# Layer A's passes two to four on half-precision parts of normalised tokens

## The chip, the core and the metric

The kernel runs on one core of one Trainium2 chip. A core has TensorE (PE in the profile; PEld is its loading of weights), VectorE (DVE), ScalarE (ACT), GpSimd (POOL) and SyncE (SP), which here issues every transfer between the chip's memory (DRAM) and the on-chip memory (SBUF); matmuls write to PSUM banks. The metric is the device time of one execution in microseconds (us); lower is better.

## The reference

Two layers process 2048 prompt tokens and 64 sample tokens of width 1024. Each layer is

```python
h = rms_norm(x, norm_g)              # x * rsqrt(mean(x*x) + eps) * g
q, k, v, gate = split(h @ w_in)
q, k = rms_norm(q, q_g), rms_norm(k, k_g)      # per head of 64
o = attend(q, k, v, bias, valid, sinks)
x = x + (o * silu(gate)) @ w_out
```

Layer A has 16 heads of queries on two heads of keys and values; a token sees its own chunk of 64 and two chunks before it, with a bias by distance and a sink per head. Layer B has 16 heads of everything and sees eight chunks back. The outputs are the two results and the newest keys and values.

## The kernel before

**Tiles and units.** Tokens lie along the free dimension in DRAM (`x0`, 128 partitions x 8 blocks x 2112 tokens). A unit is 256 tokens (two tiles of 128); eight units hold the prompt and a ninth the sample. Layer A makes four passes (`qd` 0 to 3) over the units. A pass projects queries and gates of four heads (512 columns); pass one (`qd` 0) also projects keys and values (256 columns). That is 68 tiles in all, 17 in a pass.

**Precision.** A product is made of three matmuls of parts: high x high, high x low, low x high (`project`, L753 to L755; the sample unit has both parts in one operand, L748 and L749). In layer A the parts are 32-bit values in the matmul's reduced format (`fp32r`, written f32 in the profile's PE rows). `load_act` splits raw tokens: a cast on ACT (L634) makes the high part, a subtraction on POOL (L635) the low part. Weights are multiplied by the norm's gain and split in `load_weights` (L537 on ACT, L540 on DVE). The token's 1/rms (`rr`) is applied behind the projection, when a bank of PSUM is read (`evacuate`, `evacuate_a`). Layer B's parts are half precision (f16): tokens are multiplied by their 1/rms before the split (`token_rows`, L709, spreads them over the partitions with PE; L631 multiplies on DVE), and the weights are brought to a common size by a factor from a scan of their largest value (`scan`, L177, and `input_top`, `input_across`, `input_scales`).

**What passes share.** The parts of a unit's tokens are written to a buffer in DRAM (`xsa`) and read by the passes behind. By `KEEP` units 0 and 1 are split twice, in passes one and two, and written in the second; the other units are split and written in pass one.

**Order.** PE's instructions run in an order written out by hand. `pipeline` in `layer_a` goes through the tiles: in step i come the scores of tile i, the outputs of tile i-1, and between them pieces of the projection of tile i+3 (`filler.to`). The other engines' and SP's instructions are placed by a scheduler. Small jobs that wait (`bg`) are run between the pieces. A projection bank (`pj`, two of them) is free when `evacuate_a` has read the gate (L793) and, behind the sum of squares (L840) and the power on POOL (L844), the product of L847 has read the q part.

Of the kernel before, what the change touches and what calls it, by code (L numbers as in the profile page):

```python
# [17 lines left out]
P = 128  # L18
# [24 lines left out]
FR = 0.6  # L43
KEEP = [1, 1] + [0] * (NU - 1)

# [12 lines left out]
def hybrid_encoder_kernel(  # L58
# [97 lines left out]

    most = const([P, 84], "most")
    top = const([P, 12], "top")
    scl = const([P, 9, 4], "scl")
    gsb = const([P, 8, KC], "gsb")  # L160
    S_W, C_B, G_B, C_T = (lambda h, i=i: scl[:, h, i : i + 1] for i in range(4))
    S_WO, S_OG, C_O = (scl[:, 8, i : i + 1] for i in range(3))
# [4 lines left out]
    def scan_source(i):  # L167
        if i < 64:
            return w_in_b[i // 8, i % 8 // 2, :, i % 2, :]
        if i < 80:  # L170
            return w_o_b[(i - 64) // 8, i % 8 // 2, :, i % 2, :]
        return cv_b[2 * (i - 80) : 2 * (i - 80) + 2].rearrange("e p c h d -> p e (c h d)")

    def scan(i=None, keep=0):
        while len(pending) > keep:
            j, raw = pending.pop(0)
            r = nc.vector.tensor_reduce(  # L177
                most[:, j : j + 1], raw, axis=AX.X, op=ALU.max, apply_absolute_value=True
            )
            if r.ins.engine in bg.anchors:  # L180
                behind(r.ins, bg.anchors[r.ins.engine])
            scanned.append(j)
        if i is not None:
            raw = t("wraw", [P, 512], WB) if keep else t("scan", [P, 512], 1)
            dst = raw if i < 80 else raw.rearrange("p (e c) -> p e c", e=2)
            behind(load(dst, scan_source(i)).ins, held["last"])
            pending.append((i, raw))
# [90 lines left out]
    def input_scales(h):  # L278
        everywhere(h, row[:, 20:24])

    def output_top():
# [137 lines left out]
    x1 = dr.tile([P, KC, TOK], F32, tag="x1", name="x1")  # L419
    xs = [dr.tile([P, 2 * KC * TOK], dt, tag=n, name=n) for n, dt in (("xsa", F32), ("xsb", F16))]  # L420

# [154 lines left out]
    def load_act(  # L576
# [17 lines left out]

        if cached and dt == F16:
# [6 lines left out]
            return x  # L602
        if cached:
            for c in range(4):
                xx = t("xx", [P, 4 * OT], XN, dt)
                held["last"] = load(wide(xx[:, : 4 * T]), kept(c)).ins
                x.parts.append(parts_of(xx, T, joint))
            return x

        def fetch():  # L610
# [7 lines left out]
        def split(c):  # L618
            def fn():
# [22 lines left out]
                x.parts.append(parts)  # L642
                if cache is not None and dt == F32R:
                    store(kept(c), wide(xx[:, : 4 * T]))
                elif cache is not None and c % 2:
# [33 lines left out]

    rr = [const([P, NT + 1], f"rms{l}") for l in range(2)]  # L680

    def token_scales(unit, x, ps):
# [7 lines left out]
    def sums_to_scales(layer, tt, parts, ps):  # L690
        w = len(parts)
        for i, part in enumerate(parts):
            nc.tensor.matmul(ps[:, 2 * i : 2 * i + 2], part, ones, start=True, stop=True)
# [10 lines left out]

    def token_rows(unit):
        _, T, tiles = unit
        ps = tp_bank()
        for i, (tt, _, _) in enumerate(tiles):
            nc.tensor.matmul(  # L709
                ps[:, i * P : (i + 1) * P], rr[1][:, tt : tt + 1].to_broadcast([P, P]), ident,  # L710
                start=True, stop=True,
            )
        rows = t("rows", [P, UT], 1)
        nc.vector.tensor_scalar(rows[:, :T], ps[:, :T], HB, 1.0, op0=ALU.mult, op1=ALU.mult)
        return rows

    def row_scales(unit):
        _, T, tiles = unit
        w = len(tiles)
        tt = tiles[0][0]  # L720
        acc = t("ms", [P, 8])
        for i, (_, t0, n) in enumerate(tiles):
# [38 lines left out]

    def evacuate(layer, tt, n, ps, C, G, b=None):
        a = t("pa", [P, 384], 4)
# [7 lines left out]
        else:  # L771
            out = a
        sc = rr[layer][:, tt : tt + 1]
        for dst, src in pieces:
# [10 lines left out]

    def evacuate_a(tt, ps, C, G):
        a = t("pa", [P, 384], 4)
        b = t("pb", [P, 256], 5) if G else a[:, P : 2 * P]
        sc = rr[0][:, tt : tt + 1]
        w = 2 * P if G else P  # L790
# [285 lines left out]
    def layer_a():  # L1076
# [4 lines left out]
        def add_unit(qd, place, unit):  # L1081
# [30 lines left out]
            def take_kv(it, ps):  # L1112
                tt, t0, n = it.tile
                last = u == NU
                it.kv = pr = evacuate(0, tt, n, ps, 256, 0)
                kn, v = pr[:n, 0:128], pr[:n, 128:256]
# [15 lines left out]
            def take_qg(it, ps):  # L1132
                tt, t0, n = it.tile
                if n == P and (qd or unit is not order[0]):
                    it.pr, it.gate, norm = evacuate_a(tt, ps, 512, 256)
                else:
                    it.pr, it.gate = evacuate(0, tt, n, ps, 512, 256)
                    norm = head_norm(n, it.pr[:n, 0:256], qd > 0)
# [283 lines left out]
        def outputs(it):  # L1422
# [18 lines left out]
            finished[key] = finished.get(key, 0) + 1  # L1441

        def pipeline():
            N = len(items)
            for i in range(-3, N + 1):
# [5 lines left out]
                if 0 <= i < N:  # L1451
# [58 lines left out]
    def layer_b():  # L1510
# [4 lines left out]
        def add_unit(hp, unit):  # L1515
# [7 lines left out]
            def prefetch():  # L1523
                for j in range(NO):
                    assert finished["x1", j] == 2 or j * OT >= u * UT + T
                rows = None if hp else token_rows(unit)
                st.x[hp, u] = x = load_act(
# [680 lines left out]
```

## Time and profile before

| what | value |
|---|---|
| median of three timed runs | 2076.58 us (2071.28 to 2080.74) |
| span of the profiled execution | 2081.5 us; its own time around the span is not recorded |
| attention of layer A, first to last gate row (L1361) | 54.75 to 680.04 us |
| PE, granted clock over the span | 0.994 |
| matmul groups of L753, L754, L755 with f32 operands, 512 columns | 220.8, 203.6, 203.8 us busy |
| DMA, one queue on SP | 426.51 MB, 79.9% of 16 engines |

A row of instructions reads: line, engine, operation, what is written <- what is read, shapes, count, then busy us, mean ns of one, and the engine's idle time just before with what ended it. Matmuls overlap: a mean of 398 ns is a latency, and the pace is the distance of two starts.

### The profile page before, as it was taken

The page shows a single profiled execution, that of the slowest core. Times are in us where ns is not written, and L with a number is a line of the kernel's source. Part 1 is how long each engine was busy: PE and PEld are TensorE (multiplying, and loading weights), DVE is VectorE, ACT ScalarE, POOL GpSimd, SP SyncE. Part 2 cuts the span into 40 slices and gives each one's busy share as a digit, 9 for nine tenths or more (in the row PEclk, how much of TensorE's full clock was granted, in tenths as well). Part 3 has the DMA queues.
Part 4 walks back from the last instruction along what each step waited for, and adds up shares of the span by engine and source line. Part 5 has one row for each costly group of instructions (what it writes and reads, how often), then busy time and mean ns, then how long its engine had stood idle before and what let it go on. Part 6 is the DMA issues. An engine that isn't in the chain of part 4 may idle for free.

```text
span 2081.5 us, 40775 instructions
## 1 busy us (share of the span) xinstructions
PE 1994.4 (96%) x12814; PEld 1429.3 (69%) x12814; DVE 1405.7 (68%) x4073; ACT 1439.1 (69%) x3572; POOL 1133.0 (54%) x1529
## 2 busy tenths in 40 slices
PE   7898999999999999989999999999999999999999
PEld 6777788777888999745555555555555555557888
DVE  7666777767667555677767676676766767667542
ACT  6777888777788433367778677787877778687430
POOL 5665565454447445578556565665756656565000
PEclk9999999999999999999999999999999999999999
DMA  8878787899766666789889789797987979678763
GB/s 259 252 209 220 218 213 184 228 232 240 210 159 177 197 215 204 265 227 248 218 184 244 167 200 222 175 238 176 201 221 171 245 163 215 154 155 200 229 198 113
DMA packets 610712, 429.11 MB, mean 206 GB/s; under 512 B 404208, under 2 KB 547968, under 8 KB 610464
## 3 DMA queue, kind: packets, MB, share of 16 engines
q1 hardware_dynamic: 610496, 426.51, 79.9%
q8 instruction: 101, 1.65, 0.3%
q14 instruction: 115, 0.94, 0.1%
HBM read 257.59 MB, written 73.43 MB: 159 GB/s over the span
## 4 chain that ended last, share of the span: by engine, by line
PE 54%; DVE 8%; ACT 6%; DMA 5%; issue 4%; POOL 2%; SPq 1%; ACTq 0%; DVEq 0%; POOLq 0%
PE pj L753 9%; PE pj L755 9%; PE pj L754 9%; PE o L1840 4%; PE pj L2051 4%; PE pj L2053 4%; PE pj L2052 4%; PE sb L1678 2%; PE sb L1679 2%; PE tp L1006 1%; DMA pt<-values 1%; DVE p L1682 1%; DVE wh L540 1%; DMA wraw<-in_w_o_a_dram 1%; POOL xx L635 1%
## 5 line engine op out<-in xcount | busy, mean ns | idle before, releaser
L753 PE MATMUL pj<-wh,xx 128*128 128x512 f16 (+2 forms) x1648 | 642.5, 390 | 22.4 <-DVE pa L847 9.6
L755 PE MATMUL pj<-wh,xx 128*128 128x512 f16 (+2 forms) x1648 | 624.0, 379 | 0.6 <-POOL xx L635 0.6
L1735 POOL TENSOR_TENSOR values<-p,values 128x640 f16<-128x640 f32 (+4 forms) x256 | 327.3, 1279 | 205.5 <-ACT values L1734 199.1
L754 PE MATMUL pj<-wh,xx 128*128 128x512 f16 x1024 | 388.3, 379 | 1.3 <-DVE wh L540 1.3
L1694 ACT ACTIVATE p<-p,nm 128x640 f32<-128x640 f32 (+5 forms) x264 | 199.5, 756 | 180.0 <-DVE nm L1687 141.0
L2051 PE MATMUL pj<-xx,wh 128*128 128x264 f32 (+1 forms) x1024 | 290.5, 284 | 11.2 <-DVE res L2057 4.0
L1682 DVE CUSTOM_DVE_ANT_0 p<-sb,BT 128x640 f32<-128x640 f32 (+5 forms) x272 | 196.5, 722 | 150.2 <-PE sb L1679 129.3
L2052 PE MATMUL pj<-xx,wh 128*128 128x264 f32 (+1 forms) x1024 | 287.6, 281 | 0.0
L635 POOL TENSOR_TENSOR xx<-xraw,xx 128x528 fp32r<-128x528 f32 (+4 forms) x144 | 184.7, 1304 | 100.2 <-ACT xx L634 92.9
L754 PE MATMUL pj<-wl,xx 128*128 128x512 f32 (+1 forms) x624 | 235.4, 377 | 2.4 <-DVE wl L540 2.4
L844 POOL TENSOR_TENSOR f<-f,mhalf 128x4 f32<-128x4 f32 x182 | 186.3, 1024 | 12.2
L755 PEld LDWEIGHTS <-xx 128*128 128x128 f16 x1024 | 100.2, 98 | 123.7 <-issue 1.9
L1342 ACT ACTIVATE p<-p,nm 128x257 f32<-128x257 f32 (+2 forms) x272 | 134.4, 496 | 70.5 <-DVE nm L1331 35.8
L1495 POOL TENSOR_TENSOR o<-gt,o 128x256 f32<-128x256 f32 (+1 forms) x132 | 104.9, 794 | 142.2 <-ACT p L1342 72.0
L1734 ACT CAST values<-p 128x640 f16<-128x640 f32 (+4 forms) x256 | 168.2, 658 | 12.5 <-DMA pt<-values 6.5
L754 PEld LDWEIGHTS <-xx 128*128 128x128 f16 x1024 | 100.3, 98 | 83.5 <-issue 3.6
L753 PEld LDWEIGHTS <-xx 128*128 128x128 f16 x1024 | 100.3, 98 | 82.0 <-ACT sq L822 1.4
L1840 PEld LDWEIGHTS <-values 128*128 128x128 f16 x1344 | 123.3, 98 | 38.8 <-DMA pt<-values 2.7
L753 PEld LDWEIGHTS pj<-wh,xx 128*128 128x128 f32 x624 | 119.7, 192 | 40.3 <-issue 8.1
L2053 PE MATMUL pj<-xx,wl 128*128 128x264 f32 x512 | 145.8, 285 | 0.9 <-DVE wl L533 0.9
L1840 PE MATMUL o<-pt,values 128*128 128x256 f16 (+1 forms) x1344 | 143.7, 255 | 1.7 <-DMA pt<-values 1.3
L2053 PE MATMUL pj<-xx,wh 128*128 128x264 f16 x512 | 141.3, 276 | 1.4 <-DVE wh L530 1.4
(292 smaller groups left out, 4719.8 us busy)
## 6 DMA issues: line engine op xcount, KB each, us to landing
xx<-xsb SPq DMA_DIRECT2D x112, 512.0 KB, 4.3
xx<-xsa SPq DMA_DIRECT2D x88, 512.0 KB, 5.0
xraw<-oga SPq DMA_DIRECT2D x64, 264.0 KB, 3.6
xraw<-ogb SPq DMA_DIRECT2D x64, 264.0 KB, 4.0
xsa<-xx SPq DMA_DIRECT2D x32, 512.0 KB, 4.0
wl<-in_w_in_b_dram SPq DMA_DIRECT2D x64, 256.0 KB, 4.9
wraw<-in_w_in_b_dram SPq DMA_DIRECT2D x56, 256.0 KB, 3.5
xraw<-in_x_dram SPq DMA_DIRECT2D x40, 256.0 KB, 4.6
```

Source lines behind the costliest of these rows:

```text
L635: nc.gpsimd.tensor_tensor(lo, rv, wide(hi), op=ALU.subtract)
L753: nc.tensor.matmul(ps[:n, :C], xh, wh, start=k == 0, stop=False)
L754: nc.tensor.matmul(ps[:n, :C], xh, wl, start=False, stop=False)
L755: nc.tensor.matmul(ps[:n, :C], xl, wh, start=False, stop=k == KC - 1)
L844: nc.gpsimd.tensor_tensor(fv, fv, mhalf[:n, :H], op=ALU.pow)
L1682: mi = nc.vector.tensor_tensor_reduce(out=p[r, :nk], in0=S[r, o : o + nk], in1=b, op0=ALU.add, op1=ALU.min, scale=1.0, scalar=3e38, accum_ ...
L1694: ex = nc.scalar.activation(p[:n, :nk], p[:n, :nk], AF.Exp, scale=-1.0, bias=it.nm[:n, c : c + 1], accum_out=it.sm[:n, c : c + 1],)
L1735: lo = nc.gpsimd.tensor_tensor(two[:, :, 1, :], pv, two[:, :, 0, :], op=ALU.subtract)
L1840: nc.tensor.matmul(it.O[:, h * T + q0 : h * T + q1_], held["VH"][:, kt, h], x, start=kt == kb and not low, stop=kt == tb and low == 1,)
L2051: nc.tensor.matmul(ps[:, :OT], wh, oh, start=k == 0, stop=False)
L2052: nc.tensor.matmul(ps[:, :OT], wh, ol, start=False, stop=False)
L2053: nc.tensor.matmul(ps[:, :OT], wl, oh, start=False, stop=k == KC - 1)
```

## The change

Passes two to four read f16 parts of tokens that are already multiplied by their 1/rms. 36 conversions (nine units, four pieces of two blocks each) make these parts: a load of raw tokens, a multiply on DVE, a cast on ACT, a subtraction on POOL and a store to `xsa`, which is f16 now. `pipeline` calls one or two of them a step from the second tile on, in the order in which pass two takes the units; a unit that is not there when its load is due is converted then. Pass one splits tokens as before, but writes nothing. Two 512 KB loads of a unit's parts take the place of four.

The weights of passes two to four are scanned on the chip, one of 24 pieces a step, for their largest value; `first_top`, `first_across` and `first_scales` make the factor for a pass. The weights are split into f16 with gain times factor, and the projection's bank is read with a constant in place of the token's scale. A smaller on-chip scratch for dynamic transfers makes room.

```diff
-KEEP = [1, 1] + [0] * (NU - 1)
...
+        if i >= 84:
+            return w_qg_a[(i - 76) // 8, (i - 84) % 8 // 2, :, i % 2, :]
...
+    def first_top(q):
+        a = 76 + 8 * q
+        mv = most[:, a : a + 8]
+        nc.vector.tensor_tensor(mv, mv, gain[:, 0, :], op=ALU.mult)
+        largest(10 + q, a, a + 8)
+
+    def first_across(q):
+        ps = tp_bank()
+        nc.tensor.transpose(ps[0:1, 0:P], top[:, 10 + q : 11 + q], ident)
+        m, e, r, o = (row[:, 48 + i : 49 + i] for i in (0, 1, 2, 4))
+        nc.vector.tensor_reduce(m, ps[0:1, 0:P], axis=AX.X, op=ALU.max)
...
+    def first_scales(q):
+        ps = tp_bank()
+        nc.tensor.matmul(
+            ps[:, 0:2], ones[0:1, 0:1].to_broadcast([1, P]), row[:, 52:54], start=True, stop=True
+        )
+        nc.vector.tensor_copy(scl[:, 8 + q, 0:2], ps[:, 0:2])
+        times(gsa[:, q], gain[:, 0, :], scl[:, 8 + q, 0:1])
...
-        if cached:
-            for c in range(4):
-                xx = t("xx", [P, 4 * OT], XN, dt)
-                held["last"] = load(wide(xx[:, : 4 * T]), kept(c)).ins
...
-                if cache is not None and dt == F32R:
-                    store(kept(c), wide(xx[:, : 4 * T]))
...
+    def convert(unit, c):
+        u, T, tiles = unit
+        o, joint = u * UT, T == TS
+        if c == 0 and held.get("rowed") != u:
+            rows_of(unit)
+
+        def fn():
+            raw = t("yraw", [P, 2 * UT], 2)[:, : 2 * T].rearrange("p (k s) -> p k s", k=2)
+            ld = load(raw, x0[:, 2 * c : 2 * c + 2, o : o + T])
+            behind(ld.ins, held["last"])
+            nc.vector.tensor_tensor(
+                raw, raw, held["rows"][:, :T].unsqueeze(1).to_broadcast([P, 2, T]), op=ALU.mult
+            )
+            both = t("x16", [P, 4 * UT], 3, F16)
+            xh, xl = parts_of(both, T, joint)
+            hi, lo = (xh[:, :, :T], xh[:, :, T:]) if joint else (xh, xl)
+            nc.scalar.copy(hi, raw)
+            nc.gpsimd.tensor_tensor(lo, raw, hi, op=ALU.subtract)
+            a = o * 2 * KC + 4 * c * T
+            store(xs[0][:, a : a + 4 * T], both[:, : 4 * T])
...
-                cache = None if qd < KEEP[u] else xs[0]
-                st.x[qd, u] = x = load_act(x0, u * UT, T, sums, T == TS, lead, cache, qd > KEEP[u])
+                if qd:
+                    while ("x", u) not in known:
+                        converts(1)
+                    st.x[qd, u] = x = load_act(x0, u * UT, T, False, T == TS, None, xs[0], True, F16)
+                    return x
+                st.x[qd, u] = x = load_act(x0, u * UT, T, sums, T == TS, lead)
...
-                    (st.w[qd],), _, st.emit[qd] = load_weights(0, (w_qg_a[qd], 512))
+                    (st.w[qd],), _, st.emit[qd] = load_weights(1, (w_qg_a[qd], 512), scale=gsa[:, qd])
...
+                sc = C_A(qd) if qd else rr[0][:, tt : tt + 1]
...
+        def ahead(i):
+            if 0 <= i < 24:
+                scan(84 + i)
...
                 filler.to(c0 + 0.3 * (end - c0))
+                ahead(i)
...
+                if i > 0:
+                    converts(1 + (i % 3 == 0))
...
-    nc = _bacc.Bacc("TRN2", target_bir_lowering=False, num_devices=1)
+    nc = _bacc.Bacc("TRN2", target_bir_lowering=False, num_devices=1, dynamic_dma_scratch_size=1024)
```

More of the change, by code (lines that the diff above doesn't have):

```diff
@@ L279, in input_scales @@
         everywhere(h, row[:, 20:24])
+    def first_top(q):
[8 more added lines that the diff above has]
+        nc.vector.tensor_reduce(m, ps[0:1, 0:P], axis=AX.X, op=ALU.max)
+        nc.vector.tensor_scalar(m, m, 1e-12, 1.0, op0=ALU.max, op1=ALU.mult)
+        powers(m, e, r)
+        times(o, r, WB_)
+        times(row[:, 53:54], e, 1 / (HB * WB_))
+    def first_scales(q):
[5 more added lines that the diff above has]
+        times(gsa[:, q], gain[:, 0, :], scl[:, 8 + q, 0:1])
+    C_A = lambda q: scl[:, 8 + q, 1:2]
     def output_top():
@@ L419, in hybrid_encoder_kernel @@
     x1 = dr.tile([P, KC, TOK], F32, tag="x1", name="x1")
-    xs = [dr.tile([P, 2 * KC * TOK], dt, tag=n, name=n) for n, dt in (("xsa", F32), ("xsb", F16))]
+    xs = [dr.tile([P, 2 * KC * TOK], dt, tag=n, name=n) for n, dt in (("xsa", F16), ("xsb", F16))]
     def wide(x):
@@ L680, in hybrid_encoder_kernel, with rows_of, converts @@
     rr = [const([P, NT + 1], f"rms{l}") for l in range(2)]
+    known = set()
+    def rows_of(unit):
+        held["rowed"] = unit[0]
+        held["rows"] = token_rows(unit, 0)
+    def convert(unit, c):
[17 more added lines that the diff above has]
+            store(xs[0][:, a : a + 4 * T], both[:, : 4 * T])
+        fn()
+    normal = []
+    def converts(n):
+        for _ in range(min(n, len(normal))):
+            unit, c = normal.pop(0)
+            convert(unit, c)
+            if c == 3:
+                known.add(("x", unit[0]))
     def token_scales(unit, x, ps):
@@ L691, in sums_to_scales @@
         w = len(parts)
+        known.update((layer, tt + i) for i in range(w))
         for i, part in enumerate(parts):
@@ L720, in row_scales @@
         tt = tiles[0][0]
+        known.update((0, tt + i) for i in range(w))
         acc = t("ms", [P, 8])
@@ L1441, in outputs @@
             finished[key] = finished.get(key, 0) + 1
+        normal.extend((unit, c) for unit in order[2:5] + order[:2] + order[5:] for c in range(4))
+        def ahead(i):
+            if 0 <= i < 24:
+                scan(84 + i)
+            elif i == 24:
+                scan()
+            q, at = divmod(i - 1, 8)
+            if i > 0 and 1 <= q <= 3:
+                if at == 0:
+                    first_top(q)
+                elif at == 1:
+                    first_across(q)
+                elif at == 2:
+                    first_scales(q)
+                    known.add(("w", q))
+            if i > 0 and normal and normal[0][1] == 0:
+                rows_of(normal[0][0])
         def pipeline():
```

37 lines of the change are left out of this document (18 added, 19 removed).

## The prediction

> **What bounds the kernel now.** I read the page's head first, then busy times by stretch (start:end, length, then busy us of PE, PEld, DVE, ACT and POOL with counts, the granted clock, the DMA share), and then who made PE wait in the two stages that the change touches. The first stage is pass one of layer A once attention runs, the second is passes two to four; 222 us is taken as the border because projections run three tiles ahead of attention, and the row of the fourteenth gated tile stands there.
>
> ```profile
> span 2081.5 us, 40775 instructions
> PE 1994.4 (96%) x12814; PEld 1429.3 (69%) x12814; DVE 1405.7 (68%) x4073; ACT 1439.1 (69%) x3572; POOL 1133.0 (54%) x1529
> ...
> 221.82 0.62 POOL L1361 TENSOR_TENSOR G<-pb,sm 128x256 f32<-128x256 f32 x1 [3.02 <-DVE sm L1359]
> ...
> 54.00:222.00 168.00, 150.66 (x935) 126.61 (x934) 110.12 (x377) 130.89 (x360) 98.12 (x147) 0.96 0.82 224
> 222.00:640.00 418.00, 409.29 (x2365) 328.85 (x2363) 297.79 (x971) 338.87 (x933) 220.95 (x380) 1.00 0.80 211
> 552.00:627.00 75.00, 75.00 (x438) 61.25 (x437) 50.59 (x174) 60.74 (x167) 36.77 (x64) 1.00 0.69 179
> ```
>
> In 222 to 640, PE is busy 409.29 of 418 us, and in 552 to 627 without a gap, while ACT, next in line, stands at 60.74 of 75 (81%). So passes two to four are bound by PE, and a shorter matmul shortens them. Pass one is looser: 17 us of gaps, and the clock at 0.96. The waits of PE (total us, times, longest), first 54 to 222, then 222 to 640:
>
> ```profile
> PE pj L753 <- DVE pa L847: 8.4, 5, 4.0
> PE pj L753 <- ACT pa L776: 4.1, 1, 4.1
> PE pj L753 <- ACT xx L634: 3.2, 1, 3.2
> ...
> PE o L1403 <- DVE pl L977: 3.9, 10, 0.5
> PE tp L1006 <- DVE pa L847: 1.3, 2, 1.1
> PE o L1403 <- ACT ph L976: 1.2, 1, 1.2
> PE o L1403 <- DMA pt<-values: 0.9, 1, 0.9
> ```
>
> Pass one loses its time where a projection bank comes free late: L847, the scaling of the normed q that reads the bank, comes after POOL's power (L844), and whatever stands ahead of it on POOL or DVE delays the next projection. In the later passes the four waits make 7.3 us.
>
> **The gain: f16 projections.** One run of twelve projection matmuls in layer A, and one in layer B, where both operands are f16 already (start, duration):
>
> ```profile
> 598.38 0.51 PE L753 MATMUL pj<-wh,xx 128*128 128x512 f32 x1
> 598.72 0.40 PE L754 MATMUL pj<-wl,xx 128*128 128x512 f32 x1
> ...
> 601.04 0.40 PE L755 MATMUL pj<-wh,xx 128*128 128x512 f32 x1
> 601.27 0.38 PE L1006 MATMUL tp<-ident,pa 128*128 128x128 f32 x2
> ...
> 1111.13 0.38 PE L753 MATMUL pj<-wh,xx 128*128 128x512 f16 x1
> 1111.35 0.38 PE L754 MATMUL pj<-wh,xx 128*128 128x512 f16 x1
> ...
> 1113.51 0.38 PE L755 MATMUL pj<-wh,xx 128*128 128x512 f16 x1
> 1113.72 0.33 PE L1678 MATMUL sb<-KB,q 128*128 128x384 f16 x1
> ```
>
> From 598.72 to 601.04 are ten starts, 0.232 us each; from 1111.35 to 1113.51 ten, 0.216. The f32 run of twelve lasts 2.89 us, which is 12 x 0.232 and 0.11 more for the switch into f32; the f16 run lasts 2.59, no more than 12 x 0.216. A tile's 24 matmuls stand in three runs, so a tile gains 24 x 0.016 + 3 x 0.11 = 0.7 us. Three passes of 16 tiles give 33 us; the sample tile's 16 matmuls add one, which I leave as rounding. The groups agree (behind the bar: busy us, mean ns of one):
>
> ```profile
> L755 PE MATMUL pj<-wh,xx 128*128 128x512 f16 x1024 | 388.4, 379 | 0.6 <-POOL xx L635 0.6
> L753 PE MATMUL pj<-wh,xx 128*128 128x512 f32 x512 | 220.8, 431 | 17.1 <-DVE pa L847 8.4 <-ACT pa L776 4.9 <-ACT xx L634 3.2
> L755 PE MATMUL pj<-wh,xx 128*128 128x512 f32 x512 | 203.8, 398 | 0.0
> ...
> L754 PEld LDWEIGHTS pj<-wl,xx 128*128 128x128 f32 x624 | 120.3, 193 | 17.5 <-DVE wl L540 3.0
> L754 PEld LDWEIGHTS <-xx 128*128 128x128 f16 x1024 | 100.3, 98 | 83.5 <-issue 3.6
> ```
>
> (52 + 19 + 19 ns over 400 triples would be 36 us.) I take **33**, bounds 31 and 36. The weight load halves, from 193 to 98 ns.
>
> The Trainium skill, "TensorE: Matmul & The Clock Gate" (Step-by-step: what each phase is for), says that a load of weights is pulled ahead under the running matmul. By that rule a load of 193 ns would hide behind a matmul of 216 ns, and the gain would be nothing. The trace disagrees: the f32 starts are 0.232 apart.
>
> **What is added.** Layer B's first pass already makes such parts; its rows price the steps. In order: multiply by the token's scale, cast, low part, scan of weights, token scales spread over partitions by PE.
>
> ```profile
> L631 DVE TENSOR_TENSOR xraw<-xraw,rows 128x512 f32<-128x512 f32 x32 | 25.5, 839 | 0.2
> L634 ACT CAST xx<-xraw 128x512 f16<-128x512 f32 x32 | 18.6, 616 | 12.3 <-DVE xraw L631 9.0 <-DVE ms L695 3.3
> L635 POOL TENSOR_TENSOR xx<-xraw,xx 128x512 f16<-128x512 f32 x32 | 40.4, 1287 | 15.1 <-ACT xx L634 15.1
> L177 DVE TENSOR_REDUCE most<-wraw 128x1 f32<-128x512 f32 x76 | 51.5, 678 | 0.3
> L709 PE MATMUL tp<-ident,rms 128*128 128x128 f32 x34 | 6.0, 299 | 2.3 <-DVE scl L228 1.9 <-DVE scrow L210 0.4
> ...
> 850.00:980.00 130.00, 119.12 (x699) 70.47 (x698) 97.30 (x255) 82.80 (x198) 96.79 (x107) 0.99 0.91 254
> 1110.00:1240.00 130.00, 129.23 (x778) 74.59 (x777) 92.80 (x277) 98.33 (x241) 81.42 (x108) 1.00 0.86 202
> ```
>
> The change makes 36 conversions (DVE 30, ACT 22, POOL 46 us) and 24 scans (DVE 16 us); it drops the second split of units 0 and 1 (8 casts, 8 low parts) from pass two. All lies beside PE except the 17 spreading matmuls (6 us at most) and three small scale pairs. What conversions cost PE through queues, layer B shows: with 36 of them in 850 to 980, PE was busy 119.12 us of 130, later 129.23. The 10 us between is my price for 36, spreading matmuls within.
>
> The pace is four conversions in three tile steps from the first step on: 17 fall in pass one, 19 in the first 14 steps of pass two. The 19 cost 19/36 of 10, **5** us. For the 17 in pass one, that price is 5 too, but ACT there goes from 130.89 to about 141 of 168 us (84%), while it had 64% in 850 to 980, and POOL gets 22 us more ahead of the L844 that frees banks. I take double, **10**; bounds 0 and 17, the last being all of today's gaps once more. Scans and scale pairs: **2**, bounds 0 and 5; the cover is DVE's spare time, 110.12 busy of 168. Queued behind a scan or multiply that waits for its load are, on DVE, the score minimum and L847, then PE.
>
> Later passes have shorter steps: ACT's 81% becomes about 88%, and the wait on pl (3.9 us today) should grow. I take **3**, bounds -3 and 8. DMA helps against that:
>
> ```profile
> xx<-xsa SPq DMA_DIRECT2D x88, 512.0 KB, 5.0
> ...
> xsa<-xx SPq DMA_DIRECT2D x32, 512.0 KB, 4.0
> ...
> xraw<-in_x_dram SPq DMA_DIRECT2D x40, 256.0 KB, 4.6
> ```
>
> 88 loads become 48, and 32 stores become 32 of half the size. New are 32 loads of 256 KB for the conversions and 24 for the scans, while 8 of the 40 loads of x go with the second split, so the sum falls by 20 + 8 - 12 = 16 MB; issues on SP stay near the same number (88 + 32 + 8 against 48 + 32 + 32 + 24), so its queue gains little. Weight splits, evacuations by a constant in place of the token's scale, and smaller scratch cost nothing here: the same instructions on the same engines, beside a PE that is late.
>
> Sum: -33 + 5 + 10 + 2 + 3 = **-13 us**. The span is 2081.5; this execution's time around it is not shown, and the three timed runs (2071.28 to 2080.74, median 2076.58) lie below it, 0.2% at the median. The terms are differences, so I take them from the median: **2063.5**.
>
> **The rivals.**
>
> *Given back in pass one* (chance 0.27). Conversions double pass one's 17 us of gaps and its clock loss (0.04 of 168 is 7), and take the 14 x 0.7 = 10 us that pass two would gain while they last: -33 + 24 + 10 = +1, about **2077**. Rows for it:
>
> ```profile
> 86.47 1.26 POOL L635 TENSOR_TENSOR xx<-xraw,xx 128x512 fp32r<-128x512 f32 x1
> ...
> 86.71 1.30 DVE L938 SCALAR_TENSOR_TENSOR pb<-sq,pb 128x256 f32<-128x256 f32 x1
> ...
> 89.56 0.76 PE L753 MATMUL pj<-wh,xx 128*128 128x512 f32 x1 [4.03 <-DVE pa L847]
> 90.12 0.63 PE L754 MATMUL pj<-wl,xx 128*128 128x512 f32 x1
> ```
>
> A low part on POOL, a DVE product that ends only after it, a bank freed late, a gap of 4.03 us, and matmuls of 0.63 us in place of 0.40 after it. The Trainium skill, "SBUF — State Buffer" (SBUF: two separate sides), gives a rule for it: a DVE instruction with two SBUF inputs and a POOL one exclude each other for the whole instruction. By that rule, the trace agrees (1.30 us at 86.71), and 36 more low parts and 36 multiplies collide more often. Against it: the split's 512 KB stores leave pass one, and with them SP's waits for POOL.
>
> *All hidden* (0.15). The background work fits into idle time, PE keeps its order, and nearly the whole 33 is seen: about **2047**. For it: the shares above stay under 90%; against: 850 to 980.
>
> *Slower: DVE held by loads* (0.05). Its place is DVE's queue: 60 new instructions (36 multiplies, 24 scans) wait for fresh transfers with L847 behind them. At 1 us of PE each the sum is -33 + 60 = +27, **2103**; it passes +0.5% from 0.72 us each. Against: 76 scans in layer B waited 0.3 us in all, 32 multiplies 0.2.
>
> *No faster pace* (0.03). If something of layer A other than its type sets 0.232, the gain is gone and about 17 us remain as cost: **2094**. Against: the weight load halves with the type.
>
> **How the numbers follow.** The forecast has 0.50, with its own range 2055 to 2070. 0.5% is 10.4 us, about what a measurement tells from no change, so the bound of faster is 2066. Faster: 0.38 of the forecast and 0.15; same: 0.12 of the forecast and 0.25 of given back; slower: 0.02, 0.05 and 0.03. The range 2046 to 2081 leaves out the slower cases, the tail of given back and part of all hidden.
>
> **What would show it.** Projections of passes two to four as f16 with starts 0.216 apart, and 552 to 627's step about 0.7 us shorter: the gain. Pass one longer by some 10 us, with more waits on L847: its price. PE's gaps in passes three and four not above 11 us: no new bound. The prediction fails if pass one grows by over 20 us, or if PE idles in passes three and four behind ACT.

## The result and the profile after

The changed kernel takes 2103.59 us (median of four runs, 2100.46 to 2108.02), the kernel before beside it 2075.13 (2071.28 to 2080.74): a ratio of 1.0142, with an interval of 1.012 to 1.0164. It is **slower**, by some 29 us, where 13 us less were forecast: the whole interval lies above 1, though by less than 2%. The time lies above the range.

The head of the page after, and its row of the parts' loads:

```profile
span 2102.1 us, 41007 instructions
...
PE 1990.2 (95%) x12857; PEld 1342.8 (64%) x12857; DVE 1454.7 (69%) x4172; ACT 1452.2 (69%) x3600; POOL 1168.9 (56%) x1557
...
xx<-xsa SPq DMA_DIRECT2D x48, 512.0 KB, 4.8
```

The change does what it says: 48 loads in place of 88, and PE has 4 us less to do. The longer span is time in which PE waits: its gaps sum to 87.1 us of the span before and 111.9 after. Busy times by stretch show where (columns as in the prediction: PE, PEld, DVE, ACT, POOL, clock, DMA share, GB/s). First after, with pass one, passes two to four, and the first 14 steps of pass two; then the same 14 steps before:

```profile
54.00:222.00 168.00, 145.99 (x908) 122.92 (x907) 123.84 (x391) 131.73 (x357) 114.27 (x155) 0.96 0.77 209
222.00:640.00 418.00, 390.47 (x2338) 236.78 (x2336) 320.41 (x1015) 334.62 (x924) 227.55 (x380) 0.98 0.67 173
235.00:363.00 128.00, 115.54 (x680) 68.81 (x679) 105.23 (x328) 100.98 (x276) 81.15 (x124) 0.96 0.79 213
```

```profile
222.00:338.00 116.00, 113.50 (x658) 91.43 (x656) 82.65 (x274) 98.96 (x269) 69.25 (x114) 1.00 0.75 196
```

The 14 steps grew from 116 to 128 us. PE went from 98% busy to 90%, while DVE went from 82.65 us (71%) to 105.23 (82%); ACT's 100.98 is hardly more than before. The granted clock of these steps fell too, from 1.00 to 0.96, but it does not order the kernels: in the same 14 steps e1 below has 0.97 and takes 115.0 us, e4 0.99 and takes 125.8. PE's waits after, 222 to 640 (total, times, longest):

```profile
PE o L1466 <- DVE pl L1034: 8.6, 9, 2.8
PE tp L1063 <- DVE sm L1422: 6.3, 1, 6.3
PE o L1466 <- DMA pt<-values: 4.1, 2, 2.3
```

The two largest end with DVE. Five rows of the timeline around the longest one, of 6.3 us (start, duration, engine):

```profile
291.09 4.88 DVE L568 SCALAR_TENSOR_TENSOR wh<-wl,gsa,wh 128x512 f16<-128x512 f32 x4
...
300.91 1.21 DVE L716 TENSOR_TENSOR yraw<-yraw,rows 128x512 f32<-128x512 f32 x1
...
302.64 0.47 DVE L904 SCALAR_TENSOR_TENSOR pa<-pj,scl,f 128x256 f32<-128x256 f32 x1
...
303.04 0.16 DVE L1422 RECIPROCAL sm<-sm 128x4 f32<-128x4 f32 x1
...
303.26 0.66 PE L1063 MATMUL tp<-ident,pa 128*128 128x128 f32 x2 [6.30 <-DVE sm L1422]
```

PE wants to transpose a tile's queries (pa) and stands still for 6.30 us. The profile names a reciprocal of 0.16 us as what released it; L904, which writes the queries themselves, ended only 0.09 us ahead of it, behind the same burst on DVE. In front of both lie, among the usual work, four low parts of weights, a scan and multiplies of tokens; from 288.00 to 303.20 DVE was busy 15.08 of 15.20 us. DVE has idle time over the stage, but not at this place.

**Stages.** The start of each tile's gate row (before L1361, after L1424) cuts layer A; these are differences of those rows in us, for the kernels whose stages the text uses. Span start to the 14th row is pass one, 14 more rows the part of pass two with conversions, 40 more the rest of layer A; behind the last row comes layer B.

| kernel | to 14th row | next 14 | next 40 | behind | span |
|---|---|---|---|---|---|
| before | 221.8 | 115.9 | 342.3 | 1401.5 | 2081.5 |
| after | 234.6 | 128.5 | 332.0 | 1407.0 | 2102.1 |
| e1, gain alone | 219.4 | 115.0 | 331.5 | 1405.8 | 2071.7 |
| e2, cost alone | 232.1 | 139.2 | 339.5 | 1400.0 | 2110.8 |
| e3, no multiply | 229.0 | 125.0 | 330.8 | 1405.5 | 2090.3 |
| e5, no multiply, no scan | 231.8 | 122.5 | 330.7 | 1402.0 | 2086.9 |
| e8, f16 without added work | 222.6 | 112.4 | 330.7 | 1408.7 | 2074.4 |
| e9, before with low parts moved | 215.7 | 115.2 | 339.7 | 1405.3 | 2075.8 |
| e10, e8 with low parts moved | 215.8 | 114.1 | 326.6 | 1400.5 | 2057.0 |

The profiled execution of before was some 8 us slower than its median, and the times behind layer A differ by up to 9 us over the same code, so small differences of this table are read with that in mind. The medians below carry the verdicts.

### The profile page after: what moved, and what is told of

Its sections match the earlier page's. It is cut to its first block, busy times and chain, and to the rows that moved or that the text cites. A ratio compares the mean times of both kernels' runs of the same rounds, so it can differ in the third digit from the quotient of the medians.

```text
span 2102.1 us, 41007 instructions
## 1 busy us (share of the span) xinstructions
PE 1990.2 (95%) x12857; PEld 1342.8 (64%) x12857; DVE 1454.7 (69%) x4172; ACT 1452.2 (69%) x3600; POOL 1168.9 (56%) x1557
## 4 chain that ended last, share of the span: by engine, by line
PE 57%; DVE 14%; ACT 9%; DMA 8%; issue 7%; POOL 5%; SPq 1%; POOLq 0%; ACTq 0%; DVEq 0%
PE pj L812 10%; PE pj L813 10%; PE pj L814 10%; PE pj L2136 4%; PE pj L2138 4%; PE pj L2137 4%; PE o L1925 4%; PE sb L1763 2%; PE sb L1764 2%; DVE p L1394 2%; PE tp L1063 2%; DMA pt<-values 1%; DVE wh L568 1%; POOL xx L656 1%; DVE o L1579 1%
## 5 line engine op out<-in xcount | busy, mean ns | idle before, releaser
L812 PE MATMUL pj<-wh,xx 128*128 128x512 f16 (+2 forms) x1648 | 626.2, 380 | 30.3 <-DVE pa L904 9.8
L814 PE MATMUL pj<-wh,xx 128*128 128x512 f16 (+2 forms) x1648 | 619.9, 376 | 0.0
L813 PE MATMUL pj<-wh,xx 128*128 128x512 f16 x1408 | 535.6, 380 | 1.3 <-DVE wh L568 1.3
L814 PEld LDWEIGHTS <-xx 128*128 128x128 f16 x1408 | 138.2, 98 | 169.0 <-issue 4.1
L656 POOL TENSOR_TENSOR xx<-xraw,xx 128x528 fp32r<-128x528 f32 (+4 forms) x136 | 177.0, 1323 | 89.1 <-ACT xx L655 82.5
L812 PEld LDWEIGHTS <-xx 128*128 128x128 f16 x1408 | 138.2, 98 | 115.9 <-issue 5.8
L813 PEld LDWEIGHTS <-xx 128*128 128x128 f16 x1408 | 138.2, 98 | 114.5 <-issue 5.7
L1394 DVE CUSTOM_DVE_ANT_0 p<-sa,BT,nsink 128x256 f32<-128x256 f32 (+2 forms) x272 | 116.2, 468 | 7.5 <-PE sa L1384 3.2
L900 POOL TENSOR_TENSOR f<-f,small 128x4 f32<-128x4 f32 x182 | 38.0, 209 | 148.0 <-DVE f L897 129.9
```

Of the source, the lines that this page charges most:

```text
L656: nc.gpsimd.tensor_tensor(lo, rv, wide(hi), op=ALU.subtract)
L812: nc.tensor.matmul(ps[:n, :C], xh, wh, start=k == 0, stop=False)
L813: nc.tensor.matmul(ps[:n, :C], xh, wl, start=False, stop=False)
L814: nc.tensor.matmul(ps[:n, :C], xl, wh, start=False, stop=k == KC - 1)
```

## The experiments

A difference in us is (ratio - 1) x 2073, the median of before in those runs (2071.73 to 2073.99 in three groups).

**Gain and cost apart.** e1 keeps the f16 projections, their loads and as many stores, and takes the work away; e2 keeps the projections of before and does all the work into a buffer that nobody reads.

```diff
 e1, from the kernel after
-            raw = t("yraw", [P, 2 * UT], 2)[:, : 2 * T].rearrange("p (k s) -> p k s", k=2)
-            ld = load(raw, x0[:, 2 * c : 2 * c + 2, o : o + T])
...
-            nc.scalar.copy(hi, raw)
-            nc.gpsimd.tensor_tensor(lo, raw, hi, op=ALU.subtract)
-            store(xs[0][:, a : a + 4 * T], both[:, : 4 * T])
+            st = store(xs[0][:, a : a + 4 * T], x16[:, : 4 * T])
...
-                scan(84 + i)
 e2, from the kernel after
-            store(xs[0][:, a : a + 4 * T], both[:, : 4 * T])
+            store(spare16[:, a : a + 4 * T], both[:, : 4 * T])
...
+                cache = None if qd < KEEP[u] else xs[0]
...
-                    (st.w[qd],), _, st.emit[qd] = load_weights(1, (w_qg_a[qd], 512), scale=gsa[:, qd])
+                    (st.w[qd],), _, st.emit[qd] = load_weights(0, (w_qg_a[qd], 512))
```

> Leaves out the conversions (a constant piece is stored in their place) and the scans (a fixed factor); projections of passes two to four are f16 as in the changed kernel, so the output is not the reference's. Theory (the cost of the background work ate the gain): PE's f16 order alone gains about 0.44 us in each of 48 tile steps, 21 us, less grown waits: 2054 to 2062. Rival (the attention chain between the projections holds the step, whatever the projections cost): passes three and four stay as long as before, 2068 to 2076.

> The kernel before, with f32 projections and its own shared parts, plus all conversions and scans of the change, whose parts go to a buffer that nobody reads. Theory (DVE is too full while the work lasts): pass one and the first 14 steps of pass two grow by 25 us or more, 2098 to 2120. Rival (the f16 steps are too short for work that the longer f32 steps would hide): 2076 to 2088.

e1: 2070.27 us, ratio 0.9991 (0.9978 to 1.0005), 2 us less than before and not told from it. e2: 2113.19, ratio 1.0198 (1.0174 to 1.0223), 41 more. So the background work costs 31 us in the changed kernel (1.0142 against 0.9991), and the gain without it is near nothing. Both are news: the forecast had 17 us of cost (10, 5 and 2) and 33 of gain. e2 minus e1's gain would give 39 where the change gave 29; e2 also moves the f32 parts (DMA 0.91 busy in pass one, after 0.77), so its 41 is no clean price of the work.

**Which work.** e3 is without the multiply of tokens and the spreading of their scales, e4 without the subtraction on POOL; e12 has a fixed factor for the weights in place of the scan, and e5 is e3 and e12 in one.

```diff
 e3 and e5, from the kernel after
-            nc.vector.tensor_tensor(
-                raw, raw, held["rows"][:, :T].unsqueeze(1).to_broadcast([P, 2, T]), op=ALU.mult
-            )
 e4
-            nc.gpsimd.tensor_tensor(lo, raw, hi, op=ALU.subtract)
 e5 and e12
+    for q in range(1, 4):
+        nc.vector.memset(scl[:, 8 + q, 1:2], 0.5 / (HB * WB_))
+        times(gsa[:, q], gain[:, 0, :], 2 * WB_)
...
-            if 0 <= i < 24:
-                scan(84 + i)
```

> Leaves out the multiply by the token's scale in the conversions, and with it the spreading of the scales (passes two to four work on tokens without that scale). DVE loses 36 instructions of about 0.8 us with their waits for the load of x; ACT, POOL and the transfers keep theirs. Theory (DVE's queue): 12 to 20 us faster than the changed kernel, 2084 to 2092. Rival (POOL's low parts ahead of the power that frees a bank): within 5 us of the changed kernel, 2099 to 2104.

> Leaves out the subtraction on POOL in the conversions; the low parts of passes two to four stay zero. Theory (DVE's queue): within 6 us of the changed kernel, 2097 to 2104. Rival (POOL's low parts, by their place ahead of the power and by the port that they share with DVE): 10 to 20 us faster, 2084 to 2093.

> Leaves out the multiply by the token's scale and also the scans (a fixed factor for the weights); conversions keep load, cast, low part and store. Theory (what costs is DVE's time and what waits in its queue): DVE is back near the load of the kernel before, 2072 to 2081. Rival (casts, low parts and transfers of the conversions carry the rest): 2084 to 2089, like the run without the multiply alone.

> The changed kernel with a fixed factor in place of the scans of weights (24 loads of 256 KB, 24 reductions of 0.68 us on DVE, three small chains left out). Theory (cost goes by DVE's time; the multiplies cost 15 us for 30 us of it): 5 to 9 us faster than the changed kernel, 2094 to 2099. Rival (scans fill idle time): 2101 to 2104.

| kernel | median us | ratio to before | us above before |
|---|---|---|---|
| after | 2103.59 | 1.0142 (1.012 to 1.0164) | 29.4 |
| e4, no low parts | 2098.50 | 1.0121 (1.0099 to 1.0144) | 25.1 |
| e12, no scan | 2092.98 | 1.0110 (1.0084 to 1.0136) | 22.8 |
| e3, no multiply | 2088.86 | 1.0083 (1.0062 to 1.0104) | 17.2 |
| e5, neither multiply nor scan | 2082.34 | 1.0038 (1.0020 to 1.0056) | 7.9 |
| e1, none of the work | 2070.27 | 0.9991 (0.9978 to 1.0005) | -1.9 |

By the medians, DVE's share is 21.5 us of the 31.3 (29.4 to 7.9): the multiplies (with the spreading) 12, the scans 7 when taken alone and 9 between e3 and e5. POOL's 46 us of low parts cost about 4. The intervals don't separate these 4 from nothing, nor the 7 of e12; the other steps they do. Casts, low parts and loads together are the remaining 10 (e5 to e1). The time of e5 fell between its two expectations. One row of after, grouped by line from 54 to 363 us, shows the multiplies, one the scans (busy, mean ns, idle before):

```profile
L716 DVE TENSOR_TENSOR yraw<-yraw,rows 128x512 f32<-128x512 f32 (+1 forms) x36 | 26.1, 731 | 11.8 <-DMA yraw<-in_x_dram 11.7
...
L179 DVE TENSOR_REDUCE most<-scan 128x1 f32<-128x512 f32 x24 | 16.2, 675 | 0.0
```

By the medians these 42 us of DVE's time cost 21.5 of the kernel's: about half a microsecond for each, and rather less for DVE alone. With the scans go 24 loads, with the multiplies the spreading matmuls, and the wait for tokens moves to ACT, whose casts wait 9.3 us for them in e5.

The stages give DVE less. The 28th gate row stands at 363.1 us in after, 354.0 in e3, 354.2 in e5 and 334.4 in e1: 9 us for multiplies and scans, 20 for the rest. The profiled execution of e5 took 2088.70 us, 6 more than its median, so its stages may be that much too long, which doesn't close the gap. That the background work costs some 30 us is shown; that most of it is DVE's is not: its share lies between 9 us (stages) and 21 (medians).

**Is it the wait for loads?** The idle 11.7 us of that row are DVE standing at a multiply whose tokens have not landed, which is the mechanism of the rival at 2103. e11 loads the raw tokens two pieces ahead, into four buffers.

```diff
 from the kernel after
+    def fetch_raw():
+        if len(fetched) < len(pieces):
+            (u, T, _), c = pieces[len(fetched)]
+            raw = t("yraw", [P, 2 * UT], 4)[:, : 2 * T].rearrange("p (k s) -> p k s", k=2)
+            ld = load(raw, x0[:, 2 * c : 2 * c + 2, u * UT : u * UT + T])
...
+            while len(fetched) < min(n + 3, len(pieces)):
+                fetch_raw()
```

> The changed kernel with the raw tokens of a conversion loaded two pieces ahead, in four buffers in place of two. Theory (DVE's time is what costs; it stood only 12 us waiting for these loads): 0 to 8 us faster than the changed kernel, 2096 to 2103. Rival (the wait of the multiply at the head of DVE's queue for its load): 15 us faster or more, 2088 or less.

What the multiplies of e11 waited for, in the view of that line (us, times):

```profile
  DMA yraw<-in_x_dram: 4.0, 3
```

The wait fell from 11.7 us to 4.0, and the time did not fall with it: 2106.58, ratio 1.0192 (1.0158 to 1.0227). So that rival named the right time with the wrong mechanism: it had 60 instructions stand for a microsecond each, and they stood for 11.7 us in all. e11 is no clean trade, though: its multiplies took 890 ns on average in place of 731, and its casts waited 4.4 us for a store of earlier parts. What DVE costs is then rather the length of the added work in a fixed order, of which the stall of 6.30 us is one case; no run prices that apart.

**Why the gain is small.** e1 has nothing added and yet gains 2 us. Five gate rows of pass three before (a step is the distance of two rows), with the busy times of this stretch, and the same five tiles after, with theirs:

```profile
423.78 0.61 POOL L1361 TENSOR_TENSOR G<-pb,sm 128x256 f32<-128x256 f32 x1 [2.20 <-DVE sm L1359]
431.49 0.62 POOL L1361 TENSOR_TENSOR G<-pb,sm 128x256 f32<-128x256 f32 x1 [1.48 <-DVE sm L1359]
440.46 0.61 POOL L1361 TENSOR_TENSOR G<-pb,sm 128x256 f32<-128x256 f32 x1 [1.47 <-DVE sm L1359]
448.27 0.62 POOL L1361 TENSOR_TENSOR G<-pb,sm 128x256 f32<-128x256 f32 x1 [1.49 <-DVE sm L1359]
457.24 0.61 POOL L1361 TENSOR_TENSOR G<-pb,sm 128x256 f32<-128x256 f32 x1 [1.47 <-DVE sm L1359]
```

```profile
423.78:457.24 33.46, 32.87 (x191) 26.59 (x189) 23.24 (x76) 25.63 (x73) 16.18 (x28) 1.00 0.89 237
```

```profile
448.63 0.62 POOL L1424 TENSOR_TENSOR G<-pb,sm 128x256 f32<-128x256 f32 x1 [2.21 <-DVE sm L1422]
456.34 0.61 POOL L1424 TENSOR_TENSOR G<-pb,sm 128x256 f32<-128x256 f32 x1 [1.51 <-DVE sm L1422]
465.31 0.61 POOL L1424 TENSOR_TENSOR G<-pb,sm 128x256 f32<-128x256 f32 x1 [1.48 <-DVE sm L1422]
473.12 0.61 POOL L1424 TENSOR_TENSOR G<-pb,sm 128x256 f32<-128x256 f32 x1 [1.49 <-DVE sm L1422]
482.09 0.62 POOL L1424 TENSOR_TENSOR G<-pb,sm 128x256 f32<-128x256 f32 x1 [1.48 <-DVE sm L1422]
```

```profile
448.63:482.09 33.46, 32.07 (x195) 19.58 (x194) 23.23 (x76) 25.62 (x73) 16.08 (x29) 1.00 0.67 150
```

The steps are 7.71, 8.97, 7.81 and 8.97 us in both, to the hundredth, though the conversions have long ended, PE has less to do and DMA fell from 0.89 to 0.67. A step whose length doesn't move when the projections shrink is not set by them, not even with PE at 98%. DVE's and ACT's work is the same in both, and so is the step.

The Trainium skill, "Perfetto Trace Analysis" (Identifying the Most-Contended Engine), says that the busy share of matmuls is a poor measure of how near TensorE is to its limit, because matmuls are pipelined, and points to the arithmetic reached, set against the peak, and to the share of weight loads. The trace agrees on the first: 98% was no limit here. The share of weight loads does not tell the two cases apart: before, it stood at 79% in this stretch (26.59 of 33.46 us) and at 82% from 552 to 627 us (61.25 of 75), where the steps did shrink with the projections.

Rows of after within one of these steps suggest a path that leaves PE out for most of the time:

```profile
467.45 0.48 ACT L1565 ACTIVATE gt<-tp,sva 128x256 f32<-128x256 f32 x1
...
467.95 0.98 DVE L1344 SCALAR_TENSOR_TENSOR q<-tp,qf,q 64x256 f16<-64x256 f32 x2 [0.24 <-ACT gt L1565]
...
468.97 0.48 DVE L1394 CUSTOM_DVE_ANT_0 p<-sa,BT,nsink 128x256 f32<-128x256 f32 x1
...
471.74 0.51 ACT L1405 ACTIVATE p<-p,nm 128x257 f32<-128x257 f32 x1 [1.09 <-DVE nm L1400]
...
473.47 0.69 DVE L1034 TENSOR_TENSOR pl<-sa,ph 128x512 f16<-128x512 f32 x1 [0.43 <-ACT ph L1033]
```

The gate's copy on ACT holds up the low parts of queries on DVE, these the minima of the scores, these the exponents on ACT, and the outputs wait for pl. The next gate copy stands behind the exponents in ACT's order, which would close a loop. This is read from the rows; two changes of order bear on it.

**Outputs' inputs earlier.** e6 (from e1) and e7 (from before) make the values of tile i-1 ready ahead of the scores of tile i, so that ph and pl come earlier.

```diff
+                if 0 <= i - 1:
+                    values(items[i - 1])
                 if 0 <= i < N:
                     scores(items[i])
...
-                    values(items[i - 1])
```

> The run with f16 projections and no background work, with the transposes and splits of tile i-1 put ahead of the scores of tile i in PE's order. Theory (in steps of 9.0 us a loop from the scores over minimum, exponent, ph and pl back to the outputs sets the step, so that PE's gain is lost): the loop is cut, steps 28 to 50 fall from 8.45 to about 7.9 us, 8 to 14 us faster than without, 2056 to 2062. Rival (the loop is not what holds, ACT's load is): within 4 us of 2070.

> The kernel before with the same move in PE's order. Theory (loop): passes two and three can only fall to PE's f32 pace of 8.23 us a step from 8.45, 3 to 7 us faster than before, 2066 to 2070. Rival (no loop): 2072 or slower.

e6: 2092.58, ratio 1.0092 (1.0066 to 1.0117); e7: 2089.09, ratio 1.0078 (1.0051 to 1.0105). Both are slower than the kernels that they start from; this theory fell. The steps became even, and no shorter than the mean of 8.37 (33.46 / 4): seven gate rows of e7 from 428.86 to 479.23 are 8.40 apart. In e6 new waits stand at the head of PE's list, 222 to 640:

```profile
PE o L1459 <- DMA pt<-values: 14.9, 10, 4.2
PE tp L1056 <- DVE nm L1393: 6.2, 10, 1.2
```

**f16 without any added work.** e8 changes the kernel before: all four passes use f16 parts of raw tokens with a fixed power of two on the weights, and the token's scale stays at the reading of the bank.

```diff
 from the kernel before
-    xs = [dr.tile([P, 2 * KC * TOK], dt, tag=n, name=n) for n, dt in (("xsa", F32), ("xsb", F16))]
+    xs = [dr.tile([P, 2 * KC * TOK], dt, tag=n, name=n) for n, dt in (("xsa", F16), ("xsb", F16))]
...
+    times(gsa, gain[:, 0, :], WB_)
...
+    rs = (WB_ * WB_, 1.0)
...
-                    (st.w[qd],), _, st.emit[qd] = load_weights(0, (w_qg_a[qd], 512))
+                    (st.w[qd],), _, st.emit[qd] = load_weights(1, (w_qg_a[qd], 512), scale=gsa)
```

> The kernel before with f16 parts in all four passes of layer A, from raw tokens, a fixed factor of 2 to the 14 for the weights, and the token's scale where the bank is read, as before: no conversions, no scans, no added instructions. Theory: the gain without cost, with the loop in place: about the run with f16 projections alone, plus 5 us in pass one, 2060 to 2068. Rival (f16 projections do not shorten any pass): 2071 to 2076.

2073.39, ratio 1.0002 (0.9985 to 1.0019). With the pace in four passes and no added work, there is still no gain by the median; the last 40 steps take 330.7 us, as in e1 and e5. So the small gain is not the work's doing.

Median and stages don't agree on how small it is. The last gate row of layer A stands at 680.0 us in before, 665.9 in e1 and 665.7 in e8, so f16 seems worth 14 us there, while the medians show 2 and 0. Part of the 14 belongs to the one profiled execution of before, 8 us above its median: its last 40 steps take 342.3 us, those of e2 and e9, which also run f32 steps there, 339.5 and 339.7. And behind layer A e1 and e8 take 4 and 7 us more than before. With one profile for each kernel this stays open.

**The loop's order on DVE.** e9 (from before) and e10 (from e8) place the low parts of queries (`lows`) ahead of the gate's copy.

```diff
             if it is not None:
                 queries(it, tp[:, : 2 * n])
+                lows(it)
             if done is not None:
                 done.gt = gate_t(
...
-            if it is not None:
-                lows(it)
```

> The kernel before, with the low parts of the queries (DVE) put ahead of the copy of the gate (ACT) that follows on the same bank. Theory (passes two and three are held by a loop in which ACT and DVE wait for each other: exponents, gate copy, low parts of the queries, score minima, exponents): the loop gets 0.5 us shorter, steps 33 to 46 fall from 8.4 to PE's 8.25 us, 2 to 6 us faster than before. Rival (PE holds these steps, or another loop): within 2 us of before.

> The kernel with f16 parts in all passes and no added work, with the same move. Theory (loop of ACT and DVE): here PE would allow 7.8 us a step, so steps 33 to 46 fall from 8.4 to about 8.0, 6 to 12 us faster than without the move, 2061 to 2068. Rival (another loop holds): 2071 to 2076.

e9: 2075.64, ratio 1.0022 (1.0006 to 1.0038), no gain with f32 parts and if anything a loss. e10: 2062.18, ratio 0.9959 (0.9943 to 0.9976): below both kernels, and 9 us below before. Three gate rows of e10 in pass three:

```profile
429.65 0.61 POOL L1364 TENSOR_TENSOR G<-pb,sm 128x256 f32<-128x256 f32 x1 [1.48 <-DVE sm L1362]
437.96 0.61 POOL L1364 TENSOR_TENSOR G<-pb,sm 128x256 f32<-128x256 f32 x1 [1.48 <-DVE sm L1362]
446.26 0.61 POOL L1364 TENSOR_TENSOR G<-pb,sm 128x256 f32<-128x256 f32 x1 [1.48 <-DVE sm L1362]
```

The steps are even, 8.3 us, where PE alone needs 7.8 (below). So the order matters, but in this stretch the step fell by only 0.06 us (from a mean of 8.37), where taking the gate's copy (0.48 us) out of the loop was to save 0.5. Over steps 33 to 46, which the expectations name, the mean fell from 8.23 (e8) to 8.07, and with f32 parts from 8.34 (before) to 8.14 (e9). Of the 17 us between the spans of e8 and e10, 7 come in pass one, 4 in the last 40 steps and 8 behind layer A, where the code is the same, while the next 14 steps take 2 more; the medians differ by 11. That the faster pace and the moved low parts gain only together is shown for the whole time, not for a stage: in its trace e9 is 6 us shorter than before in pass one, too. What holds the step at 8.3 us no run tests. Rows of e10 name a candidate:

```profile
436.57 0.51 ACT L1345 ACTIVATE p<-p,nm 128x257 f32<-128x257 f32 x1 [1.06 <-POOL p L1332]
...
439.75 0.95 ACT L1277 ACTIVATE q<-tp,qf 64x256 f16<-64x256 f32 x2
...
440.73 0.98 DVE L1284 SCALAR_TENSOR_TENSOR q<-tp,qf,q 64x256 f16<-64x256 f32 x2 [0.40 <-PE sa L1324]
...
444.64 0.27 DVE L1340 TENSOR_SCALAR nm<-nm 128x1 f32<-128x1 f32 x2
...
444.88 0.51 ACT L1345 ACTIVATE p<-p,nm 128x257 f32<-128x257 f32 x1 [1.07 <-DVE nm L1340]
```

From 436.57 us ACT works with no gap over 0.03 us from the second pair of exponents to the queries (q), 4.16 us; from 440.73 DVE works in the same way from their low parts to the last minima, 4.15 us, and then the next exponents start. The two make 8.31 us, the step. The row at 440.73 names PE's last score as what DVE waited for, and it came within 0.1 us of ACT's q, so a path through the outputs and scores on PE is about as long.

## Why the prediction was wrong, step by step

The prediction's terms by stage, in us, beside the table's differences of after and before:

| term | forecast | measured |
|---|---|---|
| pass one: conversions 10, scans 1 | +11 | +12.8 |
| first 14 steps of pass two: gain -10, conversions 5, scans 1 | -4 | +12.6 |
| the rest: gain -23, stalls 3 | -20 | -10.3 |
| behind layer A | 0 | +5.5 |
| sum | -13 | +20.6 |

The medians differ by 28.5; the 8 us between are the profiled execution of before, slower than its median. The forecast had seen that gap (0.2%) and added its terms to the median, rightly.

**"I take 33, bounds 31 and 36" (the gain).** Failed, twice over. First the size: 0.7 us a step counted 0.11 us for each of three switches into f32, read from the long distance between the first two matmuls of a run. The f32 run starts sooner behind what precedes it, so that most of this comes back. Transposes followed by projections, after and then before:

```profile
600.53 0.60 PE L1063 MATMUL sa<-ident,p 128*128 128x128 f32 x4
600.96 0.38 PE L812 MATMUL pj<-wh,xx 128*128 128x512 f16 x1
601.18 0.38 PE L813 MATMUL pj<-wh,xx 128*128 128x512 f16 x1
```

```profile
598.03 0.60 PE L1006 MATMUL sa<-ident,p 128*128 128x128 f32 x4
```

From the transposes to the second projection matmul are 0.65 us after and 0.69 before (598.03 to 598.72): f16 saves 0.04 there, not 0.11. At the step's other two runs it saves 0.02 (behind the transposes of the gate, 601.49 to 601.95 before and 603.77 to 604.21 after) and 0.01 (behind scores, 595.83 to 596.17 and 598.47 to 598.80). With the pace of the other 21 matmuls, 21 x 0.016 = 0.34, that makes 0.41. Steps of pass four in which PE never waits show it, four before and four after:

```profile
578.05 0.61 POOL L1361 TENSOR_TENSOR G<-pb,sm 128x256 f32<-128x256 f32 x1
...
610.92 0.61 POOL L1361 TENSOR_TENSOR G<-pb,sm 128x256 f32<-128x256 f32 x1
```

```profile
589.80 0.61 POOL L1424 TENSOR_TENSOR G<-pb,sm 128x256 f32<-128x256 f32 x1
...
620.99 0.61 POOL L1424 TENSOR_TENSOR G<-pb,sm 128x256 f32<-128x256 f32 x1
```

These are 32.87 us, 8.22 a step, and 31.19, 7.80 a step. The difference is 0.42, so 48 steps are worth 20 us, not 33.

Second the place: "so passes two to four are bound by PE" was read from a share of 98%. In pass three another limit lay at 8.37 us a step, 0.15 above PE's 8.22, and faster matmuls met it at once. The 40 last steps gained 10.3 us, 0.26 each (8 against the f32 steps of e2 and e9). The sign stood in the prediction's own fence: ten waits of the outputs for DVE's pl, 3.9 us. They were priced as a stall that may grow by 3, not as the end of a loop that sets the step.

**"10" for conversions in pass one.** Right in sum, with 12.8 for 11. e1 shows that the stage without the work is 15.2 us shorter than after and 2.4 shorter than before, so the gross price was 15, within its bounds of 0 to 17. But the doubling that gave the 10 had no row of its own, so that the size came out is partly luck, and the sign that was named did not show. Waits on L847's product, which is L904 after, did not grow: 9.7 us before (8.4 and 1.3), 8.4 after (6.3 and 2.1). New are waits that the profile puts down to DVE's minima of the scores (0.2 us before), from 54 to 222:

```profile
PE pj L812 <- DVE nm L1400: 6.6, 4, 2.7
PE pj L812 <- DVE pa L904: 6.3, 2, 4.7
```

**"19/36 of 10, 5" for pass two.** Failed most, in sign: after against e1 the stage costs 13.5. The price came from layer B's first pass, where DVE is busy 97.30 us of 130 (75%). In pass two DVE rose to 82%, as the conversions meet weight parts there (the 4.88 us at 291.09). For this stage the prediction checked no engine's share; the queue that filled was DVE's. How much of the 13.5 is DVE's is not settled: without multiplies and scans the stage still takes 122.5 us (e5), 7.5 more than e1.

**"2" for scans, bounds 0 and 5, cover "DVE's spare time".** Failed by the medians: 7 us alone (e12, within the noise), 9 beside kernels without the multiply (e5 against e3, clear of it). Their stages don't show it (354.2 and 354.0 us to the 28th gate row). Spare time as an average is no cover in an order written out by hand; the 6.30 us stall is what it looks like.

**"3" for stalls in the later passes.** Not a sum of stalls: the loss is the loop, in the gain's term above. From the 28th gate row to the 62nd, PE's gaps went from 6.2 us (before, 338 to 627, 282.80 of 289) to 12.2, just above the 11 that the prediction set as a sign; after:

```profile
363.00:644.00 281.00, 268.85 (x1623) 162.45 (x1621) 205.45 (x667) 227.84 (x636) 143.74 (x253) 0.99 0.60 151
```

**The rivals.** *Given back in pass one* put 24 us into pass one and only the lost gain of 10 into pass two; they measured 12.8, and 12.6 beyond the lost gain. *DVE held by loads* had the time, 2103 for 2103.59, by luck: e11 takes its mechanism away. *No faster pace* falls with the step of 7.80 us in pass four. *All hidden* is what e1 was built to be: it took 2070, so even then 2047 was out of reach.

## What to carry to other kernels

Before a faster instruction on the busiest engine is counted, look for the second limit: take the steps' lengths in several stages, and the short repeated waits, because an engine at 98% can sit 0.15 us in front of a loop through two others. Price background work at the fullest in-order queue that it enters, in the stage where that queue also has its own bursts; here a microsecond of work added to DVE, 71% busy before and 82% after, cost up to half a microsecond of the kernel. If a conversion can keep its scale at the place where results are read anyway (e8, e10, with a fixed factor on the weights), the faster type comes without the work; here it paid only with a change of order (e10).

## What the hardware showed that was not expected

A long distance between the first two matmuls of a run need not be a switch that costs time. Behind four transposes the first f32 projection starts 0.35 us after theirs (598.03 to 598.38) and the first f16 one 0.43 (600.53 to 600.96); the second follows 0.34 and 0.22 later. Behind two transposes the first comes at 0.14 and 0.22 us, behind scores at 0.03 and 0.11, so an f32 run starts 0.08 us sooner each time and loses it, with 0.01 to 0.04 more, by its second matmul. The f16 distances are only the pace of what precedes: two transposes take 0.22 us also where two more follow (603.55 to 603.77), and four take twice that. Why an f32 run starts so, no run here shows.

DVE and POOL hold each other up within one instruction. A multiply of after took 1.55 us, where the median of its 36 was 0.688:

```profile
289.37 1.25 POOL L1420 TENSOR_TENSOR values<-p,values 128x512 f16<-128x512 f32 x1 [1.88 <-ACT values L1419]
...
289.61 1.55 DVE L716 TENSOR_TENSOR yraw<-yraw,rows 128x512 f32<-128x512 f32 x1
...
290.58 1.05 POOL L1424 TENSOR_TENSOR G<-pb,sm 128x256 f32<-128x256 f32 x1
```

POOL's product ends at 290.62, the multiply 0.54 us later, and the product that POOL begins meanwhile takes 1.05 us where most take 0.61. The Trainium skill, "SBUF — State Buffer" (SBUF: two separate sides), has such a pair exclude each other for a whole instruction, where the one on POOL reads SBUF; the trace agrees nearly, as 0.54 us is a little less than a whole multiply. The four low parts of weights at 291.09 took 1.22 us each, where the median of this row is 0.744, beside low parts of tokens on POOL at 292.34 and 294.21. How much of DVE's price is this, no run separates.
